# A hybrid decoder block on one Trainium2 core: later low parts, other pairs without blocks and a reordered end in the first feed-forward product

## The chip, the cores and the metric

The kernel runs on one core of a Trainium2 chip. The metric is the device time of one execution in microseconds; a run is one execution, and the time of a kernel is the median of its runs. The engines are named as the profile names them: PE is TensorE, DVE VectorE, ACT ScalarE, POOL GpSimd, and SP is SyncE, whose queue triggers most DMAs.

## What is computed

The block is a token mixer (retention and dilated attention, gated and merged) followed by a feed-forward network, each with a residual. The change lies in the feed-forward part alone, for 1024 tokens, a width of 1024 and 4096 hidden columns:

```python
def squared_relu_mlp(h, w1, w2):
    return jnp.square(jax.nn.relu(h @ w1)) @ w2

h = modulate(rms_norm(x, norm2_g[l]), sh2, sc2)
x = x + g2[:, None, :] * squared_relu_mlp(h, w_ff1[l], w_ff2[l])
return rms_norm(x, norm_f_g)
```

## The kernel before

**Split numbers.** Every operand of a matmul is split into a high part (rounded to TensorE's fast 32-bit type) and a low part (the rest). The high part is a copy on ScalarE, the low part a subtraction on VectorE, which needs the copy. One block product then takes three matmuls for each 128 rows (`mm3`, lines 219, 221 and 223): low weight by high input, high by low, high by high. Since line 219 comes first, a block product starts only when the low part of the weight is there.

**Seven products instead of eight.** `Blocks` (line 232 on) computes a 2 by 2 block product with seven block products and sums of blocks. For the first feed-forward matrix the 4096 hidden columns are worked through as 16 pairs `q` of 128 + 128 columns, and each pair needs seven products in the order 11, s1, s3, s2, 12, 22, s4 (`ORDER`). A product is 12 matmuls of 128x128 by 128x512. The names with an s use sums of weight blocks (`fs`, line 261, on VectorE).

For a product, `prep` forms the weight: the sum on VectorE if there is one, the copy of the high part on ScalarE (line 266), and the low part on VectorE (line 276), which is not issued at once but held in `self.low` until `flush`. `mm` issues the matmuls; `post` takes the result out of PSUM (line 298 a copy on ScalarE, lines 305 to 310 on VectorE, and `f_out` at lines 2218 to 2222, which adds, applies relu and squares). Product 22 adds into the PSUM bank that s3 has written and that the post of s2 must have read first (line 306 or 310).

`run` goes through `items`, the list of (pair, product): matmuls, then `prep` for as many later products as there are free tiles, then a flush, then `post`, then the callback `after`. The post of s2 is in `ahead`: it comes before the preps, and the flush is left out in the item before it. The order on each engine is the order of the code; nothing reorders it.

**ff1.** The first products of pairs 0 and 1 are woven into the normalisation of the second half of the tokens, and their inputs `t1`, `22`, `t3`, `t2`, `t4` (tiles `xt`) are formed between them. Then `run` takes the rest: (2, 11), (2, s1), then product 22 of pairs 0 and 1, whose input `t4` is the last to be formed, then (2, s3) and on to (15, s4).

**The second matrix** takes its inputs, the hidden activations `a`, from DRAM. Part of it works by blocks again: for these pairs `a_sums` (lines 2237 to 2242) forms sums of the activations on VectorE, four steps in two parts for each pair, and four pairs are one strip `c` of `xs_d`; three strips (`NS`) make 12 pairs, 0 to 11. The four other pairs, 12 to 15, are stored plainly in `a_d` and multiplied without blocks. `pack` orders the rows of the second matrix to match.

**The end of ff1.** While pair 15 runs, `second_ahead` prepares the head of the second product: `b_load(i)` triggers two loads `b{i}0`, `b{i}1` of its inputs, `b_x` splits them (line 2410 the high part on ScalarE, line 2406 the low part on VectorE), `b_raw` loads weights, `b_w` forms and splits weight sums (`w2s`, line 2448). `x1_load` (line 2104) reloads the residual into `x1r` tiles. All these loads are triggered by SP, in order; a trigger whose buffer is not free holds back those behind it. The tile tag `g0` with eight buffers serves the raw weights of ff1, its outputs `a` and the x1 tiles alike, so an x1 load can have to wait until an output is stored.

Of the kernel before, what the change touches and what calls it, by code (L numbers as in the profile page):

```python
# [133 lines left out]
def block_kernel(ctx, tc, io, stop=None, dbg=None):  # L134
# [103 lines left out]
    class Blocks:  # L238
# [79 lines left out]

        def run(self, items, sums, before=lambda q, n: None, after=lambda q, n: None, ahead=()):

            items_ahead = lambda i: i + 1 < len(items) and items[i + 1][1] in ahead
            for i, (q, n) in enumerate(items):
                before(q, n)
                self.mm(q, n)
                if n in ahead:
                    self.post(q, n)
                while sums and len(self.slots) > 1:
                    self.prep(sums.pop(0))  # L330
                if not items_ahead(i):
                    self.flush()
                if n not in ahead and n != "s1":
                    self.post(q, n)
                after(q, n)
# [1846 lines left out]

    NS = 3
    a_d = {t: dram.tile([P, S], F32, name=f"ad{t}") for t in range(8 * NS, 2 * NQ)}
# [26 lines left out]
    def f_out(q, n, x, y=None):  # L2211
# [11 lines left out]
        if n in ("12", "21"):  # L2223
            r = M["out", q][i]
            if q >= 4 * NS:
                nc.sync.dma_start(a_d[2 * q + i], r)
            elif i == 0:
                nc.sync.dma_start(xs_d[q // 4][:, 0, q % 4], r[:, :512])
            else:
                nc.sync.dma_start(xs_d[q // 4][:, 1:3, q % 4], r.rearrange("p (t x) -> p t x", t=2))  # L2230

    def a_sums(q, part):
# [11 lines left out]
        nc.sync.dma_start(xs_d[q // 4][:, 3 + 2 * part:5 + 2 * part, q % 4], r)  # L2244

# [18 lines left out]
    def ff1(ahead):  # L2264
# [71 lines left out]
        BF.post(0, "12")  # L2336
        BF.post(1, "s2")
        l()
        low = t4(3)
        BF.post(0, "s4")  # L2340
        low()
# [30 lines left out]

        BF.run(items, sums[3:], before, after, ("s2",))
        x1_load(6, x1_d)
# [97 lines left out]
    def second_ahead(n):  # L2472
# [241 lines left out]
def pack(x, c, w_ada, b_ada, norm1_g, w_in, rel_bias, ret_gn_g, ret_gn_b,  # L2714
# [51 lines left out]
```

## Time and profile before

| what | us |
|---|---|
| median of 3 runs (2180.87 to 2184.65) | 2182.93 |
| the profiled execution | 2182.82 |
| its span, from the first to the last instruction | 2181.1 |
| PE busy | 2147.4 (98%) |
| DVE busy | 1479.0 (68%) |
| ACT busy | 947.1 (43%) |
| mean granted clock of TensorE | 0.998 |

The first matmul of ff1 starts at 1534.34 us in the profiled execution, the first of the second matrix at 1848.91. A row of the timeline has the start in us, the duration, the engine, the line and operation, output and inputs by the program's names with their numbers left out, the shape, and in brackets the idle time before it and what ended it. Matmuls overlap, so the distance from start to start tells their pace, not the duration. In a row of the waits stand the total, the number of times and the longest. A row of the table of windows gives the window, its length, the busy time of PE, PEld (weight loads), DVE, ACT and POOL with the number of instructions, the granted clock of TensorE as a share of full speed, the DMA share and GB/s. SPq rows are triggers of DMAs; their second number is the time that SP spent on them, with its waits.

### The profile page before, as it was taken

Reading aid. Unit: us, or ns where it says so; the run is one execution under the profiler, and the core shown is the slowest. Engines: PE = TensorE matmul, PEld = TensorE weight load, DVE = VectorE, ACT = ScalarE, POOL = GpSimd, SP = SyncE. Lnnn points to the kernel's source line nnn. Section 1 sums busy time; section 2 is a strip of 40 time slices with the busy share of each in tenths; the row PEclk is TensorE's granted clock in tenths of the full one; section 3 lists DMA queues with packets and bytes.
Section 4 is the critical chain, followed back from the end, with each engine's and each line's share of the span. In section 5 each row is a group of like instructions: output and inputs, shape, how many; then the busy total and the mean of one; then the engine's idle time right before and its main releaser. Section 6 shows DMA issues by size and latency. Waiting matters only on the chain.

```text
span 2181.1 us, 27045 instructions
## 1 busy us (share of the span) xinstructions
PE 2147.4 (98%) x10034; PEld 1784.6 (82%) x10034; DVE 1479.0 (68%) x2281; ACT 947.1 (43%) x1715; POOL 178.4 (8%) x192
## 2 busy tenths in 40 slices
PE   7999999999999999999999999999999999999998
PEld 5888888888888888888888888888878888788887
DVE  6756777767566678854655644677876665887855
ACT  4533322333334566654644525434554455433412
POOL 0101111100000334410000000001000000000003
PEclk9999999999999999999999999999999999999999
DMA  9869998734687758977323366653054445645322
GB/s 382 231 193 297 289 328 266 217 136 155 223 297 287 257 181 242 263 222 186 105 81 108 98 250 210 224 184 130 35 202 159 154 143 188 240 138 173 109 87 78
DMA packets 161891, 422.55 MB, mean 194 GB/s; under 512 B 27734, under 2 KB 55645, under 8 KB 157662
## 3 DMA queue, kind: packets, MB, share of 16 engines
q1 hardware_dynamic: 151902, 372.57, 48.4%
q0 software_dynamic: 9856, 48.24, 10.1%
q8 instruction: 79, 1.29, 0.2%
q14 instruction: 54, 0.44, 0.1%
HBM read 325.71 MB, written 160.32 MB: 223 GB/s over the span
## 4 chain that ended last, share of the span: by engine, by line
PE 90%; DVE 4%; ACT 2%; DMA 1%; issue 1%; POOL 0%; SPq 0%; POOLq 0%; DVEq 0%; ACTq 0%
PE qap L219 6%; PE qap L223 6%; PE qap L221 6%; PE fp L219 4%; PE fp L223 4%; PE fp L221 4%; PE ak L219 2%; PE ak L221 2%; PE ak L223 2%; PE f2a L221 2%; PE f2a L223 2%; PE f2a L219 2%; PE rg L221 1%; PE rg L219 1%; PE rg L223 1%; PE va L221 1%
## 5 line engine op out<-in xcount | busy, mean ns | idle before, releaser
L219 PE MATMUL qap<-hh,qaw 128*128 128x512 f32 x264 | 102.8, 389 | 0.1
L221 PE MATMUL qap<-hl,qaw 128*128 128x512 f32 x264 | 102.7, 389 | 0.0
L223 PE MATMUL qap<-hh,qaw 128*128 128x512 f32 x264 | 102.7, 389 | 0.0
L656 POOL TENSOR_TENSOR j<-qk,j 128x512 fp32r<-128x512 f32 x32 | 48.3, 1513 | 311.7 <-ACT j L655 311.7
L2117 POOL TENSOR_TENSOR accnf<-accnf,sqnf 128x256 f32<-128x256 f32 (+1 forms) x18 | 16.6, 921 | 613.2 <-ACT sqnf L2116 613.2
L2221 ACT ACTIVATE a<-a 128x512 f32<-128x512 f32 x48 | 30.3, 632 | 78.0 <-DVE a L2220 78.0
L219 PEld LDWEIGHTS qap<-hh,qaw 128*128 128x128 f32 x264 | 49.6, 188 | 10.8 <-DVE qat L310 0.5
L221 PEld LDWEIGHTS qap<-hl,qaw 128*128 128x128 f32 x264 | 49.5, 188 | 10.3
L223 PEld LDWEIGHTS qap<-hh,qaw 128*128 128x128 f32 x264 | 49.6, 188 | 10.3
L2410 ACT CAST w2h<-w2s 128x512 fp32r<-128x512 f32 x36 | 22.4, 621 | 78.2 <-DVE w2s L2448 78.2
L2117 POOL TENSOR_TENSOR accn<-accn,sqn 128x512 f32<-128x512 f32 x12 | 15.5, 1294 | 496.0 <-ACT sqn L2116 496.0
L276 DVE TENSOR_TENSOR fw<-w1r,fw 128x512 fp32r<-128x512 f32 x48 | 32.9, 688 | 33.2 <-ACT fw L266 33.2
L1531 ACT ACTIVATE P<-P,ng 128x128 f32<-128x128 f32 (+1 forms) x96 | 41.9, 438 | 29.5 <-DVE ng L1528 29.5
L276 DVE TENSOR_TENSOR qaw<-wa,qaw 128x512 fp32r<-128x512 f32 x66 | 45.0, 686 | 11.1 <-ACT qaw L266 11.1
L1309 DVE SCALAR_TENSOR_TENSOR cossin<-cossin,cb 128x1024 f32<-128x1024 f32 x32 | 39.0, 1220 | 16.4 <-DMA cossin<-in_w_ada_dram 16.4
L219 PE MATMUL fp<-h2h,fw 128*128 128x512 f32 x128 | 50.0, 390 | 0.0
L1955 DVE TENSOR_TENSOR rwl<-rwl,rwh 128x1024 fp32r<-128x1024 f32 x25 | 30.2, 1221 | 29.0 <-ACT rwh L1985 29.0
L221 PE MATMUL fp<-h2l,fw 128*128 128x512 f32 x128 | 49.8, 389 | 0.0
L223 PE MATMUL fp<-h2h,fw 128*128 128x512 f32 x128 | 49.8, 389 | 0.0
L219 PE MATMUL roa<-rh,rwl 128*128 128x512 f32 x128 | 49.8, 389 | 0.0
L221 PE MATMUL roa<-rl,rwh 128*128 128x512 f32 x128 | 49.8, 389 | 0.0
L223 PE MATMUL roa<-rh,rwh 128*128 128x512 f32 x128 | 49.8, 389 | 0.0
(3093 smaller groups left out, 7138.1 us busy)
## 6 DMA issues: line engine op xcount, KB each, us to landing
cossin<-in_w_ada_dram SPq DMA_DIRECT2D x32, 512.0 KB, 5.3
v<-vd SPq DMA_DIRECT2D x32, 512.0 KB, 5.7
w1r<-in_w_ff_dram SPq DMA_DIRECT2D x32, 512.0 KB, 4.8
vd<-vo SPq DMA_DIRECT2D x24, 512.0 KB, 6.3
xsd<-as SPq DMA_DIRECT2D x24, 512.0 KB, 2.8
w2r<-in_w_ff2s_dram SPq DMA_DIRECT2D x24, 512.0 KB, 7.6
em<-in_w_ada_dram SPq DMA_DIRECT2D x16, 512.0 KB, 10.2
wrvs<-in_w_rv_dram POOLq DMA_DIRECT2D x16, 512.0 KB, 11.1
```

The source lines that it names most:

```text
L219: nc.tensor.matmul(o, wl, xh, start=first, stop=False, skip_group_check=skip)
L221: nc.tensor.matmul(o, wh, xl, start=False, stop=False, skip_group_check=skip)
L223: nc.tensor.matmul(o, wh, xh, start=False, stop=last, skip_group_check=skip)
L276: nc.vector.tensor_sub(t[:, 512:], src, fv(t[:, :512]))
L656: nc.gpsimd.tensor_sub(t[:, 1], src, fv(t[:, 0]))
L1309: nc.vector.scalar_tensor_tensor(t, t, 1.0, cb, op0=ALU.mult, op1=ALU.mult, accum_out=mods[:, j:j + 1])
L1531: nc.scalar.activation(v, v, AF.Exp, bias=ng[:, blk:blk + 1], accum_out=st[:, g, blk, 2 + a:3 + a])
L1955: nc.vector.tensor_sub(lo, fv(lo), fv(hi))
L2117: (nc.vector if f == 7 else nc.gpsimd).tensor_add(G["acc", key], G["acc", key], sq)
L2221: nc.scalar.activation(o, o, AF.Relu)
L2410: nc.scalar.copy(hi, src)
```

## The change

Four things, all around `ff1`. First, `run` gets a flag `lazy`: while there are sums left to prepare, the flush behind a product is left out, so that a low part is issued on VectorE behind the copy for the next weight. Second, the weight of (2, s2) is prepared before `run`, and the list of items starts with four products of pair 2 (11, s1, s3, s2) ahead of product 22 of pairs 0 and 1. Third, the pairs without blocks are 0, 1, 14 and 15, by `Q0 = 2`; pairs 2 to 13 make up the strips. Fourth, around the end the x1 loads are triggered one at a time during pairs 14 and 15, `b_load(1)` comes behind product 12 of the last pair, `b_load(2)` ahead of the last two x1 loads, and `b_x(0, .)` and half of `b_w(1, .)` later.

```diff
@@ run
-                if not items_ahead(i):
+                if not items_ahead(i) and not (lazy and sums):
                     self.flush()
@@
-    NS = 3
+    NS, Q0 = 3, 2
@@ f_out
-            if q >= 4 * NS:
-                nc.sync.dma_start(a_d[2 * q + i], r)
+            c, m = divmod(q - Q0, 4)
+            if not 0 <= c < NS:
+                nc.sync.dma_start(a_d[2 * q + i + (8 * NS if q < Q0 else 0)], r)
             elif i == 0:
-                nc.sync.dma_start(xs_d[q // 4][:, 0, q % 4], r[:, :512])
+                nc.sync.dma_start(xs_d[c][:, 0, m], r[:, :512])
...
@@ ff1
         BF.post(1, "s2")
+        BF.prep((2, "s2"))
         l()
         low = t4(3)
+        BF.flush()
         BF.post(0, "s4")
...
-        items = sums[:2] + [(0, "22"), (1, "22")] + sums[2:]
+        items = sums[:4] + [(0, "22"), (1, "22")] + sums[4:]
...
-            if q == NQ - 1 and n in ("s2", "12"):
-                for f in range(3):
-                    x1_load(f + 3 * (n == "12"), x1_d)
-
-        late = {(0, "22"): (0, 0), (1, "22"): (1, 0), (2, "s2"): (0, 1), (2, "12"): (1, 1)}
-        late.update({(q + 1, n): (q, part) for q in range(2, 4 * NS) for part, n in enumerate(("11", "s1"))})
+            f = {(2, "s2"): 0, (2, "12"): 2, (1, "s3"): 4, (1, "s2"): 1, (1, "12"): 3, (1, "22"): 5}.get((NQ - q, n))
+            if f is not None:
+                x1_load(f, x1_d)
+
+        late = {(q + 1, n): (q, part) for q in range(Q0, Q0 + 4 * NS) for part, n in enumerate(("11", "s1"))}
...
-        BF.run(items, sums[3:], before, after, ("s2",))
+        BF.run(items, sums[4:], before, after, ("s2",), True)
+        b_load(2)
         x1_load(6, x1_d)
         x1_load(7, x1_d)
         b_x(1, 0)
@@ second_ahead
         elif n == "s3":
             b_raw(0, "22", 1)
+        elif n == "s2":
             b_x(0, 0)
+        elif n == "12":
+            b_load(1)
             b_x(0, 1)
-        elif n == "12":
-            for p in range(4):
-                b_w(1, p)
+            b_w(1, 0)
+            b_w(1, 1)
         elif n == "22":
-            b_load(1)
+            b_w(1, 2)
+            b_w(1, 3)
@@ ff2_blocks
             if i == 0:
-                b_load(2)
@@ pack
-        "w_ff2": _k4(A(w_ff2)[0, 3072:]),
-        "w_ff2s": _quads(A(w_ff2)[0, :3072]),
+        "w_ff2": _k4(np.concatenate([A(w_ff2)[0, :512], A(w_ff2)[0, 3584:]])),
+        "w_ff2s": _quads(A(w_ff2)[0, 512:3584]),
```

The number of instructions on each engine stays the same. Line numbers behind the change are two to six higher. Three places show what moves.

VectorE, at the turn to pair 2, up to the post of (2, s2) at lines 309 and 310. `fw2s3` is the weight of product s3 of pair 2, `fs` a weight sum, `a0` to `a3` the outputs of pairs 0 and 1, `as` the sums of `a_sums`, `xt` the inputs, `ft2nacc` the post. Both listings follow the same row, the output step of a3 that reads `ft1h2t`; before, 24 rows lie from it to line 310, and these are the last 12 of them:

```order
L276 TENSOR_TENSOR fw311_13380<-w1r31_13320,fw311_13380 128x512
L2220 TENSOR_TENSOR a1_13284<-fp03_13211,ft0nsq_13046 128x512
L2237 TENSOR_TENSOR as00_13387<-a0_13283 128x512
L2238 SCALAR_TENSOR_TENSOR as00_13387<-as00_13387,a1_13284 128x512
L261 TENSOR_TENSOR fs3_13403<-w1r32_13322 128x512
L276 TENSOR_TENSOR fw3s1_13405<-fs3_13403,fw3s1_13405 128x512
L2220 TENSOR_TENSOR a3_13301<-fp13_13224,ft1nsq_13067 128x512
L2237 TENSOR_TENSOR as10_13412<-a2_13300 128x512
L2238 SCALAR_TENSOR_TENSOR as10_13412<-as10_13412,a3_13301 128x512
L261 TENSOR_TENSOR fs3_13403<-w1r32_13322,w1r31_13320 128x512
L309 TENSOR_TENSOR ft2nacc_13348<-ft2nacc_13348,fp22_13432 128x512
L310 TENSOR_TENSOR ft2nacc_13349<-fp23_13416,ft2nacc_13348 128x512
```

Now 14 rows, the first six and the other eight:

```order
L261 TENSOR_TENSOR fs2_13035<-fs2_13035,w1r21_12901 128x512
L276 TENSOR_TENSOR fw2s3_13071<-fs2_13035,fw2s3_13071 128x512
L2261 TENSOR_TENSOR xt42_13293<-x1_5_12199,xt42_13293 128x512
L2326 SCALAR_TENSOR_TENSOR x1_7_12201<-x1_7_12201,mods_73 128x512
L276 TENSOR_TENSOR fw2s2_13306<-fs2_13035,fw2s2_13306 128x512
L2220 TENSOR_TENSOR a0_13283<-ft0nsq_13046,fp01_13123 128x512
```

```order
L2261 TENSOR_TENSOR xt43_13311<-x1_7_12201,xt43_13311 128x512
L2220 TENSOR_TENSOR a2_13300<-ft1nsq_13067,fp11_13136 128x512
L276 TENSOR_TENSOR fw212_13342<-w1r21_12901,fw212_13342 128x512
L261 TENSOR_TENSOR fs2_13035<-fs2_13035,w1r21_12901 128x512
L276 TENSOR_TENSOR fw222_13344<-w1r22_12941,fw222_13344 128x512
L276 TENSOR_TENSOR fw2s4_13364<-fs2_13035,fw2s4_13364 128x512
L309 TENSOR_TENSOR ft2nacc_13347<-ft2nacc_13347,fp22_13383 128x512
L310 TENSOR_TENSOR ft2nacc_13348<-fp23_13367,ft2nacc_13347 128x512
```

The sums `as00` and `as10`, the second output steps of a1 and a3 and the work for pair 3's weights (`fs3`, `fw3s1`, `fw311`) are no longer ahead of line 310; the low parts of (2, s3) and (2, s2) stand near the front.

VectorE during the last pair; `w2l` is a low part of the second matrix's first weights, `b00l` and `b01l` its first inputs. Before:

```order
L2406 TENSOR_TENSOR w2l02_15309<-w2r0111_15239,w2h02_15308 128x512
L2406 TENSOR_TENSOR w2l03_15313<-w2r0111_15239,w2h03_15312 128x512
L2406 TENSOR_TENSOR b00l_15278<-b00l_15278,b00h_15331 128x1024
L309 TENSOR_TENSOR ft15nsq_15274<-ft15nsq_15274,fp152_15343 128x512
L310 TENSOR_TENSOR ft15h2t_15275<-fp153_15316,ft15nsq_15274 128x512
L2220 TENSOR_TENSOR a31_15359<-ft15h2t_15275,fp151_15284 128x512
L2448 TENSOR_TENSOR w2s00_15383<-w2r0210_15282,w2r0220_15299 128x512
L2406 TENSOR_TENSOR b01l_15280<-b01l_15280,b01h_15334 128x1024
```

Now:

```order
L2410 TENSOR_TENSOR w2l02_15313<-w2r0111_15242,w2h02_15312 128x512
L309 TENSOR_TENSOR ft15nsq_15278<-ft15nsq_15278,fp152_15339 128x512
L310 TENSOR_TENSOR ft15h2t_15279<-fp153_15322,ft15nsq_15278 128x512
L2220 TENSOR_TENSOR a31_15355<-ft15h2t_15279,fp151_15288 128x512
L2410 TENSOR_TENSOR w2l03_15317<-w2r0111_15242,w2h03_15316 128x512
L2410 TENSOR_TENSOR b00l_15282<-b00l_15282,b00h_15359 128x1024
L2452 TENSOR_TENSOR w2s00_15385<-w2r0210_15286,w2r0220_15303 128x512
L2410 TENSOR_TENSOR b01l_15284<-b01l_15284,b01h_15382 128x1024
```

The post of (15, s2), the rows of `ft15nsq` and `ft15h2t`, has moved ahead of the low part of `b00l`.

SP's queue at the end of ff1; `x1r_6` is an x1 load, `b10l` a load of an input of the second matrix, `ad31` a store of an output of pair 15. Before:

```order
L2104 DMA x1r_4_15365<-x1d4_254 128x1024
L2104 DMA x1r_5_15367<-x1d5_255 128x1024
L2226 DMA ad31_265<-a31_15359 128x1024
L2424 DMA b10l_15423<-xsd0_266 128x1024
L2424 DMA b11l_15425<-xsd0_266 128x1024
L2226 DMA ad30_264<-a30_15358 128x1024
L2104 DMA x1r_6_15443<-x1d6_256 128x1024
L2104 DMA x1r_7_15445<-x1d7_257 128x1024
L2424 DMA b20l_15453<-xsd0_266 128x1024
L2424 DMA b21l_15455<-xsd0_266 128x1024
```

Now:

```order
L2104 DMA x1r_1_15337<-x1d1_251 128x1024
L2104 DMA x1r_3_15362<-x1d3_253 128x1024
L2428 DMA b10l_15378<-xsd0_266 128x1024
L2428 DMA b11l_15380<-xsd0_266 128x1024
L2104 DMA x1r_5_15397<-x1d5_255 128x1024
L2227 DMA ad31_265<-a31_15355 128x1024
L2227 DMA ad30_264<-a30_15354 128x1024
L2428 DMA b20l_15443<-xsd0_266 128x1024
L2428 DMA b21l_15445<-xsd0_266 128x1024
L2104 DMA x1r_6_15447<-x1d6_256 128x1024
L2104 DMA x1r_7_15449<-x1d7_257 128x1024
L2404 DMA w2r0120_15457<-in_w_ff2s_dram 128x1024
```

`b10l` and `b11l` stand ahead of both stores, `b20l` and `b21l` behind the stores and ahead of `x1r_6` and `x1r_7`.

More of the change, by code (lines that the diff above doesn't have):

```diff
@@ L317, in post, with run @@
                 self.out(q, "12", u, d)
-        def run(self, items, sums, before=lambda q, n: None, after=lambda q, n: None, ahead=()):
+        def run(self, items, sums, before=lambda q, n: None, after=lambda q, n: None, ahead=(), lazy=False):
             items_ahead = lambda i: i + 1 < len(items) and items[i + 1][1] in ahead
@@ L2224, in f_out @@
             r = M["out", q][i]
-            if q >= 4 * NS:
-                nc.sync.dma_start(a_d[2 * q + i], r)
+            c, m = divmod(q - Q0, 4)
+            if not 0 <= c < NS:
+                nc.sync.dma_start(a_d[2 * q + i + (8 * NS if q < Q0 else 0)], r)
             elif i == 0:
-                nc.sync.dma_start(xs_d[q // 4][:, 0, q % 4], r[:, :512])
+                nc.sync.dma_start(xs_d[c][:, 0, m], r[:, :512])
             else:
-                nc.sync.dma_start(xs_d[q // 4][:, 1:3, q % 4], r.rearrange("p (t x) -> p t x", t=2))
+                nc.sync.dma_start(xs_d[c][:, 1:3, m], r.rearrange("p (t x) -> p t x", t=2))
     def a_sums(q, part):
@@ L2243, in a_sums @@
                                            op1=ALU.subtract)
-        nc.sync.dma_start(xs_d[q // 4][:, 3 + 2 * part:5 + 2 * part, q % 4], r)
+        c, m = divmod(q - Q0, 4)
+        nc.sync.dma_start(xs_d[c][:, 3 + 2 * part:5 + 2 * part, m], r)
     BF = Blocks("f", X, ["g1"] * 4 + ["att*"] * 4 + ["att"] * 2 + ["att*"] * 2 + ["wh", "wl"] * 3,
```

## The prediction

> **What bounds the kernel now.** I read the page first: its busy table and its chain that ended last.
>
> ```profile
> span 2181.1 us, 27045 instructions
> PE 2147.4 (98%) x10034; PEld 1784.6 (82%) x10034; DVE 1479.0 (68%) x2281; ACT 947.1 (43%) x1715; POOL 178.4 (8%) x192
> PE 90%; DVE 4%; ACT 2%; DMA 1%; issue 1%; POOL 0%; SPq 0%; POOLq 0%; DVEq 0%; ACTq 0%
> ```
>
> TensorE carries 98% of the span and the chain runs through it for 90%. The diff changes no matmul, so it can only give back time in which TensorE stood still or ran slowly. Next I asked who TensorE waited for in the stretch that the diff touches, from the first feed-forward matmul (1534 us) to the third product of the second (1881 us):
>
> ```profile
> PE fp L219 <- DVE ft2nacc L310: 3.3, 1, 3.3
> PE f2a L221 <- DVE b21l L2406: 1.1, 1, 1.1
> PE fp L219 <- DVE ft15h2t L310: 0.8, 1, 0.8
> PE n21ss L381 <- DVE accn L2117: 0.3, 1, 0.3
> ```
>
> No other row stands there, and the last one, of the norm, is untouched. So a handful of microseconds is all that can be won. What a stall costs is read from start to start, because matmuls overlap. The clean pace: pair 9's product s1 starts at 1717.21 and its s2, two products or 24 matmuls later, at 1722.65, so 0.227 us for a matmul and 2.72 us for a product of 12.
>
> ```profile
> 1710.53 0.69 DVE L276 TENSOR_TENSOR fw9s<-fs,fw9s 128x512 fp32r<-128x512 f32 x1 [0.67 <-ACT fw9s L266]
> 1717.21 0.39 PE L219 MATMUL fp<-xt10h,fw9s 128*128 128x512 f32 x1
> 1722.65 0.39 PE L219 MATMUL fp<-xt,fw9s 128*128 128x512 f32 x1
> ```
>
> The large stall, in the timeline of TensorE, and the granted clock behind it, in the table of windows:
>
> ```profile
> 1589.34 0.39 PE L223 MATMUL fp<-h2h,fw 128*128 128x512 f32 x1
> 1593.02 0.50 PE L219 MATMUL fp<-xt,fw 128*128 128x512 f32 x1 [3.29 <-DVE ft2nacc L310]
> ...
> 1594.40 0.63 PE L223 MATMUL fp<-xt,fw 128*128 128x512 f32 x1
> ...
> 1597.39 0.48 PE L219 MATMUL fp<-x220h,fw2s 128*128 128x512 f32 x1
> 1597.71 0.39 PE L221 MATMUL fp<-x220l,fw2s 128*128 128x512 f32 x1
> 1575.00:1589.00 14.00, 14.00 (x63) 11.58 (x63) 10.82 (x18) 10.05 (x18) 0.00 (x0) 1.00 0.34 128
> 1594.40:1597.00 2.60, 2.60 (x8) 2.01 (x7) 1.94 (x4) 2.57 (x5) 0.00 (x0) 0.50 0.13 46
> ```
>
> From 1589.34 to 1597.71 are 14 matmul starts, 8.37 us where 14 x 0.227 = 3.18 would do: **5.19 us lost**. 3.45 of it is the wait itself (3.68 less one pace); the other 1.74 is the clock, granted at 0.50 for 2.6 us after it, when the starts come 0.43 apart.
>
> The Trainium skill has a rule for this ("TensorE: Matmul & The Clock Gate", Part 1: The HAM clock gate): after about one idle window of some 3.4 us the array falls to half clock, and a like time of activity brings it back. The 0.50 row behind the 3.68 us gap agrees; the return 4.4 us after the restart does too.
>
> **The change, part by part.**
>
> *(a) The stall at pair 2.* TensorE waited at product (2, 22) for L310, the step of VectorE that reads that PSUM bank. VectorE was simply late:
>
> ```profile
> 1573.91 0.69 DVE L2220 TENSOR_TENSOR a<-fp,ft1h2t 128x512 f32<-128x512 f32 x1
> ...
> 1577.82 0.68 DVE L261 TENSOR_TENSOR fs<-fs,w1r 128x512 f32<-128x512 f32 x1
> 1578.42 0.69 DVE L276 TENSOR_TENSOR fw2s<-fs,fw2s 128x512 fp32r<-128x512 f32 x1
> 1580.67 0.69 DVE L276 TENSOR_TENSOR fw2s<-fs,fw2s 128x512 fp32r<-128x512 f32 x1 [1.57 <-ACT fw2s L266]
> ...
> 1592.27 0.69 DVE L310 TENSOR_TENSOR ft2nacc<-fp,ft2nacc 128x512 f32<-128x512 f32 x1
> 1575.97 0.39 PE L219 MATMUL fp<-xt,fw 128*128 128x512 f32 x1
> ```
>
> Between a3's step (1573.91) and L310 VectorE has 24 rows before and 14 now: ten move behind L310 (the four first steps of pair 0's and 1's block sums, two output steps, two weight sums and two low parts of pair 3). Rows follow each other at 0.60 us (1577.82 to 1578.42), so L310 moves up by 10 x 0.60 = 6.0 us even if every wait for ScalarE stays, such as the 1.57 in the row of 1580.67. It then ends at 1592.96 - 6.0 = 1587.0 or sooner; TensorE arrives at 1589.34 + 0.23 = 1589.57. Margin at least 2.6 us: the wait goes, and with it the slow clock. Its own input is no hindrance: (2, s2) is now the fourth product and ends two products after 1575.97, at 1581.4. Term: **-5.19**. If the cover failed by 1 us, 1 us would come back.
>
> What is late next is the third product. Products (0, 22) and (1, 22) now follow (2, s2), so at 1575.97 TensorE needs the low part of (2, s3) instead. In the row order it stands second behind a3's step: 1573.91 + 2 x 0.60 + 0.69 = 1575.80. Margin 0.17 us, the tightest place of the change. (2, s2), due at 1578.69, has its low part three rows later; 1.0 us of margin if ScalarE's copy comes in time, and 0.4 us for the bank that the output step behind it frees. No row of before shows this order, so bounds: from 0 to the wait if the low part stayed at its place of before, 1578.42 + 0.69 - 1575.97 = 3.14 us. I take 0.1, because the rows ahead of it are all short steps whose inputs are there. Term: **+0.1** (0 to 3.1).
>
> *(b) Low parts one product later, everywhere.* With `lazy`, a low part is no longer flushed in the product that copied its high part but behind the next copy, about one product (2.72 us) later, so that VectorE no longer stands waiting for ScalarE. The rows above give the cover: pair 9's s2 has its low part at 1710.53 + 0.69 = 1711.22 and TensorE reads it at 1722.65, 11.4 us later. 8.7 us remain. Term: **0**; if the cover were gone, each of 13 pairs would wait.
>
> *(c) Which pairs go without blocks.* Pairs 0, 1, 14, 15 now, 12 to 15 before: the eight sum steps of VectorE leave pairs 0 and 1, whose VectorE is late, and come back in pairs 12 and 13. Pairs 2 to 11 carried the same steps before, and the waits above show no wait of TensorE there. The stores stay as many bytes. Term: **0** besides what (a) counts.
>
> *(d) The end of the stage.* Two places, both on VectorE's row order and on SP's queue:
>
> ```profile
> 1840.71 1.23 DVE L2406 TENSOR_TENSOR b00l<-b00l,b00h 128x1024 fp32r<-128x1024 f32 x1 [4.44 <-ACT b00h L2410]
> 1842.57 0.69 DVE L310 TENSOR_TENSOR ft15h2t<-fp,ft15nsq 128x512 f32<-128x512 f32 x1
> 1842.10 0.39 PE L223 MATMUL fp<-h2h,fw 128*128 128x512 f32 x1
> 1843.32 0.50 PE L219 MATMUL fp<-xt,fw 128*128 128x512 f32 x1 [0.83 <-DVE ft15h2t L310]
> 1843.65 0.40 PE L221 MATMUL fp<-xt,fw 128*128 128x512 f32 x1
> ...
> 1859.79 0.39 PE L219 MATMUL f2c<-b10h,w2l 128*128 128x512 f32 x1
> 1860.58 0.40 PE L223 MATMUL f2c<-b10h,w2h 128*128 128x512 f32 x1
> 1861.51 0.39 PE L219 MATMUL f2c<-b11h,w2l 128*128 128x512 f32 x1
> 1862.32 0.40 PE L223 MATMUL f2c<-b11h,w2h 128*128 128x512 f32 x1
> 1872.77 0.39 PE L219 MATMUL f2a<-b21h,w2l 128*128 128x512 f32 x1
> 1874.57 0.40 PE L223 MATMUL f2a<-b21h,w2h 128*128 128x512 f32 x1
> ```
>
> At (15, 22) TensorE loses 1843.65 - 1842.10 - 2 x 0.227 = 1.10 us, because L310 stood behind b00l's low part, and that behind a load. Now L309 and L310 stand ahead of b00l; they can start when (15, s2) ends, one product (2.72 us) before (15, 22), and need 1.4: margin 1.3. Term: **-1.10**. At b10l, b11l and b21l the same sum gives 0.34, 0.36 and 1.35 us. Their loads in SP's queue:
>
> ```profile
> 1837.43 6.33 SPq L2104 DMA_DIRECT2D x1r<-x1d  x6
> ...
> 1852.61 0.38 SPq L2424 DMA_DIRECT2D b10l<-xsd  x1
> ...
> 1853.94 0.38 SPq L2226 DMA_DIRECT2D ad<-a  x1
> 1855.29 6.45 SPq L2104 DMA_DIRECT2D x1r<-x1d  x2
> 1861.84 0.38 SPq L2424 DMA_DIRECT2D b20l<-xsd  x1
> ```
>
> b20l was issued at 1861.84 because SP had stood 6.45 us at x1r_6 and x1r_7, whose buffers are free only when pair 15's output is stored. It now goes ahead of them, directly behind that store: about 1854.4, 7.4 us earlier, for 1.35 us of lateness. b10l and b11l move ahead of both stores of pair 15 and are asked for one product sooner; only 0.34 and 0.36 are wanted. Term: **-2.05**. Late next would be x1r_6 and x1r_7, issued 0.9 us later behind the two b loads; the step that first reads them stands behind b21l's low part on VectorE, so they cannot bring that stall back. The six other x1 loads took 6.33 us of SP in one row and now go one by one. Two of them stand ahead of b00l: 2.1 us at that rate, 6.5 at that of x1r_6 and x1r_7. b00l's low part ended at 1841.94, and the second matrix starts two products after 1843.32, at 1848.8, so 6.9 us cover both ends: 0. The weight sums of the second product, which trade places with output steps, are due a whole product (10.9 us, four blocks) after that: 0.
>
> Sum: -5.19 + 0.1 - 1.10 - 2.05 = **-8.24**. The profiled execution took 2182.82 us (span 2181.1 and 1.7 around it), 0.11 below the median of the three runs; against that median the forecast is 2182.93 - 8.2 = **2174.7 us**.
>
> **The rivals.**
>
> *A new wait at (2, s3).* For it: a margin of 0.17 us, and a copy on ScalarE ahead of the next low part. Against it: only two short steps stand ahead. Full price 3.1 us, 2177.8; if a wait of that length brought the slow clock in the row's proportion (5.19 to 3.45), 4.7 us, 2179.4.
> By the clock rule named above a wait under 3.4 us costs only itself, which would give the first of the two figures.
>
> *The end of the stage keeps its stalls.* For it: the same bytes go through the same queue in the same 30 us, and b00l, b10l wait for a landing and not only for their issue. Then only (a) counts: 2182.9 - 5.1 = 2177.8.
>
> *The change does not do what it says at pair 2:* if VectorE is held by the waits for ScalarE or for pair 3's weights and not by its count of rows, L310 stays late. Then only (d) counts: 2182.9 - 3.15 = 2179.8. Against it: the ten rows are behind L310 in the program itself.
>
> *Slower.* The low parts come so late that TensorE waits for one in each of the 13 pairs from 3 on, at s2, whose low part now follows the copy of 12. One step of VectorE late (0.69 us) costs 13 x 0.69 = 9.0 us and gives 2183.7; two steps, 17.9 us and 2192.6. It decides from 8.2 / 13 = 0.63 us a pair. Against it stand 8.7 us of margin in each.
>
> **How the numbers follow.** Forecast 0.73; a new wait of over 1 us 0.08; the end kept 0.09; pair 2 kept 0.05; slower 0.03; others 0.02. A measurement of this kernel tells 0.2%, 4.4 us, from no change. Faster by more than that are the forecast, the end kept, and most of the new waits: 0.87. Within it: pair 2 kept and the rest of the waits, 0.09. Slower 0.04. Low end: all 8.3 us and the lowest run's 2.1 below the median, 2172.5. High end: 2178.5, above the two rivals at 2177.8 and short of the one at 2179.8.
>
> **What would show it.** Right: no row for ft2nacc, ft15h2t or b21l among TensorE's waits from 1534 to 1875, no window at 0.50 in the stage, L310 of pair 2 done before 1587, starts at 0.227 through (2, s3); b20l issued right behind pair 15's stores. Wrong: a wait of fp at L219 for fw2s3 or fw2s2 near 1576 to 1579; a wait of f2a for b00l or b01l; a regular wait of some tenths once in 19 us, which would be the low parts.

## The result, and the profile after

| | before | after |
|---|---|---|
| median of the runs, us | 2182.93 (7 runs, 2180.87 to 2184.88) | 2175.77 (7 runs, 2174.99 to 2178.76) |
| profiled execution: span, us | 2181.1 | 2174.0 |
| first matmul of ff1 | 1534.34 | 1535.71 |
| first matmul of the second matrix | 1848.91 | 1843.94 |
| ff1 (between the two) | 314.57 | 308.23 |
| second matrix to the span's end | 332.19 | 330.06 |

The ratio is 0.9968, with a 95% interval from 0.9959 to 0.9977: 7.2 us, or 0.3%, faster. The prediction said 2174.7 (2172.5 to 2178.5).

In the two profiled executions ff1 has become 6.34 us shorter and what follows it 2.13, together 8.47. The span shows 7.1 of it, because ff1 started 1.37 us later in that execution, in a stretch where the programs are the same (in the fourteen profiles of this study it starts between 1534.34 and 1536.02). So the kernels below are compared by two numbers: the median over the runs, and the time from ff1's first matmul to the span's end in the profiled execution, which is 646.76 before and 638.29 after.

The page of the changed kernel, its busy table and its chain:

```profile
span 2174.0 us, 27035 instructions
PE 2144.1 (99%) x10034; PEld 1782.9 (82%) x10034; DVE 1478.5 (68%) x2281; ACT 948.3 (44%) x1715; POOL 176.8 (8%) x192
PE 94%; DVE 3%; ACT 1%; issue 0%; DMA 0%; POOL 0%; POOLq 0%; DVEq 0%; ACTq 0%
```

TensorE's busy time has fallen by 3.3 us with the same 10034 matmuls: those are the slow ones that are gone, and its share of the chain has risen from 90% to 94%. Who TensorE waits for in the stretch in which four rows stood before (1530 to 1880 us):

```profile
PE n21ss L381 <- DVE accn L2117: 0.3, 1, 0.3
```

Only the untouched row of the norm is left. The windows over the place where the clock had been at 0.50 (columns as before):

```profile
1586.00:1600.00 14.00, 14.00 (x63) 11.62 (x62) 11.18 (x18) 9.76 (x17) 0.00 (x0) 1.00 0.52 180
1600.00:1625.00 25.00, 25.00 (x112) 20.67 (x112) 18.43 (x29) 12.84 (x23) 0.00 (x0) 1.00 0.70 256
```

TensorE is busy throughout, at full clock. VectorE's rows, from a3's step to the step that pair 2's product 22 had waited for, in the timeline:

```profile
1575.28 0.69 DVE L2220 TENSOR_TENSOR a<-fp,ft1h2t 128x512 f32<-128x512 f32 x1
1575.89 0.68 DVE L261 TENSOR_TENSOR fs<-fs,w1r 128x512 f32<-128x512 f32 x1
1576.49 0.68 DVE L276 TENSOR_TENSOR fw2s<-fs,fw2s 128x512 fp32r<-128x512 f32 x1
...
1578.36 0.68 DVE L276 TENSOR_TENSOR fw2s<-fs,fw2s 128x512 fp32r<-128x512 f32 x1
...
1583.85 0.69 DVE L276 TENSOR_TENSOR fw<-w1r,fw 128x512 fp32r<-128x512 f32 x1 [3.01 <-ACT fw L266]
...
1586.44 0.68 DVE L309 TENSOR_TENSOR ft2nacc<-ft2nacc,fp 128x512 f32<-128x512 f32 x1
1587.15 0.69 DVE L310 TENSOR_TENSOR ft2nacc<-fp,ft2nacc 128x512 f32<-128x512 f32 x1
...
1607.50 0.69 DVE L309 TENSOR_TENSOR ft3nsq<-ft3nsq,fp 128x512 f32<-128x512 f32 x1 [1.12 <-PE fp L223]
1608.23 0.69 DVE L310 TENSOR_TENSOR ft3h2t<-fp,ft3nsq 128x512 f32<-128x512 f32 x1
```

And TensorE's where these are read, at (2, s3), at (2, 22) and at (3, 22):

```profile
1577.34 0.40 PE L219 MATMUL fp<-xt,fw2s 128*128 128x512 f32 x1
...
1590.98 0.39 PE L219 MATMUL fp<-xt,fw 128*128 128x512 f32 x1
...
1610.02 0.39 PE L219 MATMUL fp<-xt,fw 128*128 128x512 f32 x1
```

The low part of (2, s3) ends at 1576.49 + 0.68 = 1577.17 and is read at 1577.34: the margin of 0.17 us that was forecast, to the hundredth. L310 of pair 2 ends at 1587.84, 3.1 us ahead of its reader, though VectorE stood 3.01 us for a copy of ScalarE on the way, a wait that the prediction did not have. In pair 3 L309 already waits for TensorE and not the other way round (1.12 us in its bracket): VectorE has caught up, with 1.1 us from the end of L310 (1608.92) to the start of (3, 22).

SP's queue at the end of ff1:

```profile
1846.91 3.48 SPq L2227 DMA_DIRECT2D ad<-a  x2
1850.50 0.37 SPq L2428 DMA_DIRECT2D b20l<-xsd  x1
1851.27 0.43 SPq L2428 DMA_DIRECT2D b21l<-xsd  x1
1851.80 1.76 SPq L2104 DMA_DIRECT2D x1r<-x1d  x2
```

b20l is triggered right behind pair 15's two stores, 6.6 us after the second matrix has begun, where it had been 12.9 us (1861.84 less 1848.91). The two x1 loads behind it take SP 1.76 us instead of 6.45.

### The profile page after: what moved, and what is told of

Same layout as the page of the kernel before. It is cut to its first block, busy times and chain, and to the rows that moved or that the text cites. A ratio compares the mean times of both kernels' runs of the same rounds, so it can differ in the third digit from the quotient of the medians.

```text
span 2174.0 us, 27035 instructions
## 1 busy us (share of the span) xinstructions
PE 2144.1 (99%) x10034; PEld 1782.9 (82%) x10034; DVE 1478.5 (68%) x2281; ACT 948.3 (44%) x1715; POOL 176.8 (8%) x192
## 4 chain that ended last, share of the span: by engine, by line
PE 94%; DVE 3%; ACT 1%; issue 0%; DMA 0%; POOL 0%; POOLq 0%; DVEq 0%; ACTq 0%
PE qap L219 6%; PE qap L223 6%; PE qap L221 6%; PE fp L219 5%; PE fp L221 5%; PE fp L223 5%; PE f2a L221 2%; PE f2a L223 2%; PE f2a L219 2%; PE ak L219 2%; PE ak L221 2%; PE ak L223 2%; PE rg L221 1%; PE rg L219 1%; PE rg L223 1%; PE va L223 1%
## 5 line engine op out<-in xcount | busy, mean ns | idle before, releaser
L266 ACT CAST qaw<-wa 128x512 fp32r<-128x512 f32 x66 | 39.6, 616 | 23.7 <-PE qap L223 15.3
```

The source lines that it names most:

```text
L266: nc.scalar.copy(t[:, :512], src)
```

## The experiments

The question was not whether TensorE's waits are gone, which the profile shows, but which of the four parts removed which wait, and whether the prices that the prediction gave them hold: item order with VectorE's lighter row order -5.19, low parts later 0, other pairs without blocks 0, the end -3.15. So each part was made alone, each was left out alone, and the place with the tightest margin was loaded. "ff1 to end" is the time from ff1's first matmul to the span's end, in the one execution that was traced. Each ratio is to runs of the kernel before that were made beside it (their medians lie between 2182.87 and 2183.42).

| kernel | median (range), us | ratio to before (95%) | ff1 to end | waits of TensorE over 1 us: product, us |
|---|---|---|---|---|
| before | 2182.93 | 1 | 646.76 | (2, 22) 3.3; b21l 1.1 |
| the change | 2175.77 (2174.99 to 2178.76) | 0.9968 (0.9959 to 0.9977) | 638.29 | none |
| order alone | 2187.31 (2184.41 to 2188.45) | 1.0016 (1.0007 to 1.0026) | 650.76 | (3, 12) 2.4; (3, 22) 3.7 |
| low parts alone | 2179.18 (2178.01 to 2183.28) | 0.9982 (0.9973 to 0.9992) | 642.68 | (2, 22) 1.9 |
| pairs alone | 2182.83 (2181.29 to 2184.8) | 0.9998 (0.9988 to 1.0008) | 646.80 | (2, 22) 2.9 |
| pairs alone, loads earlier | 2180.49 (2178.93 to 2184.49) | 0.9991 (0.9981 to 1.0) | 643.86 | (2, 22) 1.2; b21l 1.7 |
| end alone | 2181.21 (2180.41 to 2183.3) | 0.9991 (0.9981 to 1.0) | 644.35 | (2, 22) 3.3 |
| without low parts | 2181.96 (2180.39 to 2184.19) | 0.9995 (0.9986 to 1.0005) | 645.99 | (3, 22) 3.7 |
| without pairs | 2181.26 (2178.4 to 2182.68) | 0.9993 (0.9983 to 1.0002) | 645.41 | (3, 22) 3.7 |
| without order | 2176.49 (2175.82 to 2177.2) | 0.9973 (0.9962 to 0.9984) | 640.07 | (2, 22) 1.6 |
| without end | 2176.82 (2175.86 to 2178.1) | 0.9972 (0.9961 to 0.9983) | 639.82 | none (b21l 0.6) |

**Order alone.** The kernel before with the fourth product ahead of product 22 of pairs 0 and 1, and its weight prepared early; the sums of pairs 0 and 1 are two products later for that.

```diff
+        BF.prep((2, "s2"))
...
-        items = sums[:2] + [(0, "22"), (1, "22")] + sums[2:]
+        items = sums[:4] + [(0, "22"), (1, "22")] + sums[4:]
-        late = {(0, "22"): (0, 0), (1, "22"): (1, 0), (2, "s2"): (0, 1), (2, "12"): (1, 1)}
+        late = {(0, "22"): (0, 0), (1, "22"): (1, 0), (2, "12"): (0, 1), (2, "22"): (1, 1)}
```

> The kernel before with one part of the change: the weight of (2, s2) is prepared ahead of the loop and products (2, s3) and (2, s2) go ahead of product 22 of pairs 0 and 1; the sums of pairs 0 and 1 stay, two products later. Theory V (VectorE's queue is late by a fixed number of rows, and each of the three parts takes rows or waits out of it): the wait at (2, 22) goes, but the sums and the weights of pair 3 that stood ahead of line 310 are still to be done, so the lateness comes back within one pair, as waits of 2 to 4 us at pair 3; total from 2180 to 2188 us. Theory O (the order alone removes the stall, since it gives line 310 two more products of time): no wait above 0.3 us in pairs 2 and 3, total 2182.9 - 5.2 = 2177.7 us.

The timelines of ScalarE and TensorE at pair 3:

```profile
1607.23 0.63 ACT L2221 ACTIVATE a<-a 128x512 f32<-128x512 f32 x1 [1.35 <-DVE a L2220]
1609.57 0.50 PE L219 MATMUL fp<-h2h,fw 128*128 128x512 f32 x1 [2.44 <-ACT ft3nsq L298]
...
1612.19 0.39 PE L223 MATMUL fp<-h2h,fw 128*128 128x512 f32 x1
1616.24 0.79 PE L219 MATMUL fp<-xt,fw 128*128 128x512 f32 x1 [3.66 <-DVE ft3h2t L310]
1616.83 0.63 PE L221 MATMUL fp<-xt,fw 128*128 128x512 f32 x1
1617.26 0.63 PE L223 MATMUL fp<-xt,fw 128*128 128x512 f32 x1
...
1621.10 0.61 PE L223 MATMUL fp<-xt,fw 128*128 128x512 f32 x1
```

Slower than before. The wait at pair 2 is gone, and VectorE's lateness comes due one pair later, twice: 2.44 us at (3, 12), by way of a copy of ScalarE (L298) that stood behind steps waiting for VectorE, such as the row of 1607.23, and 3.66 at (3, 22), followed by starts 0.43 us apart for 5 us. The item order gives VectorE no time; it puts L310 of pair 2 ahead of ten rows, and these rows now stand ahead of pair 3's.

**Low parts alone, pairs alone, end alone.** The kernel before with the flag `lazy` set; with the pairs 0, 1, 14 and 15 plain; with the new triggers at the end.

```diff
-        BF.run(items, sums[3:], before, after, ("s2",))
+        BF.run(items, sums[3:], before, after, ("s2",), True)
```

> The kernel before with the lazy flush alone. V: the waits of VectorE for ScalarE ahead of line 310 (1.57 + 0.69 + 0.74 = 3.0 us) shrink, the rows stay; the wait at (2, 22) falls from 3.45 to between 0.4 and 1.9 us and the slow clock behind it goes; total 2178 to 2180 us. O: nothing changes at pair 2, 2182.9 us.

The waits of TensorE with the low parts later and nothing else:

```profile
PE fp L219 <- DVE ft2nacc L310: 1.9, 1, 1.9
PE f2a L221 <- DVE b21l L2406: 0.8, 1, 0.8
PE f2c L221 <- DVE b10l L2406: 0.6, 1, 0.6
```

This one edit takes 1.4 us off the wait at (2, 22), behind which no slow clock follows now, and removes the wait for ft15h2t at (15, 22), where the prediction gave the whole 1.10 us to the reordered end.

```diff
-    NS = 3
+    NS, Q0 = 3, 2
...
-        late = {(0, "22"): (0, 0), (1, "22"): (1, 0), (2, "s2"): (0, 1), (2, "12"): (1, 1)}
-        late.update({(q + 1, n): (q, part) for q in range(2, 4 * NS) for part, n in enumerate(("11", "s1"))})
+        late = {(q + 1, n): (q, part) for q in range(Q0, Q0 + 4 * NS) for part, n in enumerate(("11", "s1"))}
```

> The kernel before with the other choice of pairs without blocks alone (0, 1, 14, 15). V: four sum rows of 0.6 us leave the queue ahead of line 310; the wait at (2, 22) falls from 3.45 to between 0.8 and 2.0 us, the slow clock goes; total 2178.5 to 2180 us. O: nothing changes at pair 2, 2182.9 us.

A miss: 2.86 us of wait where 0.8 to 2.0 were expected, and no gain. Three engines in the timelines of this kernel, SP's queue, ScalarE and VectorE:

```profile
1578.56 2.65 SPq L2227 DMA_DIRECT2D ad<-a  x2
1581.31 1.20 SPq L2194 DMA_DIRECT2D w1r<-in_w_ff_dram  x2
1586.24 0.62 ACT L266 CAST fw<-w1r 128x512 fp32r<-128x512 f32 x1 [1.68 <-DMA w1r<-in_w_ff_dram]
1586.89 0.69 DVE L276 TENSOR_TENSOR fw<-w1r,fw 128x512 fp32r<-128x512 f32 x1 [1.60 <-ACT fw L266]
```

VectorE has four steps fewer ahead of L310, but the time goes into waits. SP stood at two stores of pair 0 and 1 (2.65 us), the loads of pair 3's weights behind them were triggered at 1581.31 (1579.38 before; 0.76 of the 1.93 us between is ff1's later start in this execution), ScalarE waited 1.68 us for the weight, and VectorE 1.60 for ScalarE's copy. Whether the stores did it was tried next: the same kernel with the two loads of pair 3 triggered ahead of them.

```diff
+        for part in (1, 2):
+            w1_load(3, part)
         low()
         BF.post(0, "12")
...
-        for part in (1, 2):
-            w1_load(3, part)
```

> q0_only with the two loads of pair 3's weights triggered ahead of the stores of a0 and a2 on SP. W: VectorE's wait of 1.60 us for the copy of fw311 goes, the wait at (2, 22) falls from 2.86 to about 1.3 us (0.8 to 1.7), and the slow clock goes with it (2.9 us in q0_only); 2182.8 - 1.6 - 2.9 = 2178.3 us. Rival (the ten rows' worth of work decides, not the load): 2182.8 us, the wait stays at 2.9.

The waits of TensorE in it:

```profile
PE fp L219 <- DVE ft2nacc L310: 1.2, 1, 1.2
PE f2a L221 <- DVE b21l L2407: 1.7, 1, 1.7
```

The wait is 1.19 us without a slow clock behind it, as expected, so it was SP's queue that had eaten the freed steps: from ff1's first matmul L310 ends after 58.6 us in the kernel before, 58.2 with the pairs alone and 56.5 here. The time is a miss, 2180.49 where 2178.3 was expected: at the end b21l cost 1.7 us in this profile, 1.3 more than where the loads stood behind the stores. Why it grew is not settled.

```diff
-            if q == NQ - 1 and n in ("s2", "12"):
-                for f in range(3):
-                    x1_load(f + 3 * (n == "12"), x1_d)
+            f = {(2, "s2"): 0, (2, "12"): 2, (1, "s3"): 4, (1, "s2"): 1, (1, "12"): 3, (1, "22"): 5}.get((NQ - q, n))
+            if f is not None:
+                x1_load(f, x1_d)
...
+        b_load(2)
         x1_load(6, x1_d)
```

> The kernel before with the reordered end alone (x1 loads one by one, b loads earlier, b00 and b01 split later). If the stalls there come from the order of the queues: no wait at (15, 22), b10l, b11l, b21l, so 3.15 us less, 2179.8 us, with pair 2 unchanged. If they come from the bandwidth that the loads share: the waits stay, 2182.9 us.

All the waits of the end vanish and (2, 22) keeps its 3.3, as expected. From the second matrix to the span's end it takes 330.01 us instead of 332.19, the 2.1 us of the prediction. The median gained 1.7 where 3.15 were expected. In the traced execution the clock is at 0.50 for 6.8 us at the wait at (2, 22) and not for 3.4 (the windows are in the last section), which gives 1.1 us back there; whether the other executions are the same in this is not on record.

**All but one part.** The changed kernel with the flag off; with the pairs 12 to 15 plain again (the sums of pairs 0 and 1 as in order alone); with product 22 of pairs 0 and 1 ahead of (2, s3) again and the weight of (2, s2) no longer prepared ahead of the loop; with the end as before.

```diff
-        BF.run(items, sums[4:], before, after, ("s2",), True)
+        BF.run(items, sums[4:], before, after, ("s2",))
```

> The changed kernel with the lazy flush taken out again. Theory W (VectorE's queue at pair 2 is late by its rows and by its in-order waits for copies on ScalarE, which themselves wait for pair 3's weights; no part alone clears both, and what is not cleared falls due at pair 3): a wait of 2 to 4 us at (3, 22), with the slow clock behind it if it is as long as the 2.86 us of q0_only; 2.3 to 7 us over the changed kernel's 2175.8, so 2178 to 2183 us. Rival (order and choice of pairs are enough, lazy is only a reserve): 2175.8 us, no wait.

> The changed kernel with pairs 12 to 15 without blocks as before, so that the eight sum rows of pairs 0 and 1 (8 x 0.61 = 4.9 us of VectorE) stand at the start of pair 3. W: a wait of 1 to 3 us at (3, 22), 2177 to 2181 us. Rival (order and lazy are enough): 2175.8 us, no wait.

> The changed kernel with product 22 of pairs 0 and 1 ahead of (2, s3) as before. W: with the sums and most of the ScalarE waits gone line 310 is late by 0.3 to 1.5 us, without slow clock; 2176 to 2177.5 us. Rival (the order is what clears pair 2): the wait of before, 2.9 us or more with the slow clock, 2180 us or more.

Both kernels that lack one of the two parts priced at 0 lose most of the gain, at pair 3. Without the other pairs the wait is longer than the 1 to 3 us that were expected, and the time just above the range. Why is seen in VectorE's groups between 1575 and 1612 us (number, busy time and mean, then the idle time ahead of them and what ended it). In the changed kernel:

```profile
L276 DVE TENSOR_TENSOR fw<-w1r,fw 128x512 fp32r<-128x512 f32 x6 | 4.1, 687 | 4.1 <-ACT fw L266 4.1
L276 DVE TENSOR_TENSOR fw3s<-fs,fw3s 128x512 fp32r<-128x512 f32 x4 | 2.7, 686 | 0.4 <-ACT fw3s L266 0.3
```

Without the later low parts:

```profile
L276 DVE TENSOR_TENSOR fw<-w1r,fw 128x512 fp32r<-128x512 f32 x6 | 4.1, 690 | 7.7 <-ACT fw L266 7.7
L276 DVE TENSOR_TENSOR fw3s<-fs,fw3s 128x512 fp32r<-128x512 f32 x4 | 2.8, 692 | 3.5 <-ACT fw3s L266 3.5
```

Without the other pairs:

```profile
L276 DVE TENSOR_TENSOR fw<-w1r,fw 128x512 fp32r<-128x512 f32 x6 | 4.1, 685 | 3.0 <-ACT fw L266 3.0
L276 DVE TENSOR_TENSOR fw3s<-fs,fw3s 128x512 fp32r<-128x512 f32 x4 | 2.7, 686 | 0.1
L2237 DVE TENSOR_TENSOR as<-a 128x512 f32<-128x512 f32 x3 | 2.1, 685 | 0.8 <-ACT a L2222 0.8
L2241 DVE TENSOR_TENSOR as<-a,a 128x512 f32<-128x512 f32 x3 | 2.1, 685 | 1.6 <-DMA xsd<-as 1.6
```

In the one VectorE stands 7.7 + 3.5 us ahead of low parts, waiting for copies, where it stands 4.1 + 0.4 in the changed kernel; in the other it stands 3.0 + 0.1, but has the sums of pairs 0 to 2 to do (three of the first of four steps, in the row of L2237) and not those of pair 2 alone, and stands 1.6 us more ahead of the third of these steps until earlier sums are stored (L2241). Either way L310 of pair 3 is 3.7 us late, and the slow clock follows. VectorE needs both relief measures to be in time at (3, 22), and then it has the 1.1 us of margin shown above. Without the order L310 of pair 2 stands behind the steps of product 22 of pairs 0 and 1 again, and the other parts make up for all but 1.62 us of it; no slow clock follows, and 1.78 us are lost from ff1 to the end. That wait is a little longer than the 0.3 to 1.5 us that were expected; the median is in its range, and 0.7 above the changed kernel's, which is within the noise of the runs.

```diff
-            f = {(2, "s2"): 0, (2, "12"): 2, (1, "s3"): 4, (1, "s2"): 1, (1, "12"): 3, (1, "22"): 5}.get((NQ - q, n))
-            if f is not None:
-                x1_load(f, x1_d)
+            if q == NQ - 1 and n in ("s2", "12"):
+                for f in range(3):
+                    x1_load(f + 3 * (n == "12"), x1_d)
...
-        b_load(2)
         x1_load(6, x1_d)
```

> The changed kernel without its reordered end: the x1 loads again three at a time, b_load(1) and b_load(2), b_x(0, .) and b_w(1, .) where they were before; low parts, item order and pairs without blocks as in the changed kernel. Theory D (the end is worth its own term): waits of TensorE for b21l (0.6 to 1.7 us) and b10l (0.3 to 0.6) come back, from the start of the second matrix to the span's end it is 331.5 to 332.5 us where the changed kernel has 330.1, no window at half clock, time 2177.8 (2177.2 to 2178.7). The wait for ft15h2t stays away, since it was away where the low parts alone came later. Rival (the end gains only beside a late pair 2, with later low parts VectorE has room and nothing comes back): 2175.8, 330.1 us.

The waits of TensorE without the reordered end:

```profile
PE f2a L221 <- DVE b21l L2409: 0.6, 1, 0.6
```

The second matrix to the span's end takes 331.68 us, 1.6 more than in the changed kernel, and the median is 1.05 higher (2176.82, 0.4 below the range expected), with intervals that overlap. Only b21l comes back, with a wait of 0.6 us; b10l and ft15h2t do not. Of the 1.6 us, 1.1 are lost in the first 46 us of the second matrix, where b10l, b11l and b21l are read. The other 0.5 comes only in or behind the last 220 of its 1520 matmuls, and is not the end of ff1: kernels that have the reordered end show it too (330.55 us without the later low parts, 330.54 without the other pairs, where the changed kernel has 330.06). So beside later low parts the reordered end is worth about 1.1 us in the profiles, and not 3.15.

**The tightest place, loaded.** The low part of (2, s3) is subtracted one, four or six times more, with the same result, so that VectorE is late by a chosen amount at the place with 0.17 us of margin.

```diff
-                nc.vector.tensor_sub(t[:, 512:], src, fv(t[:, :512]))
+                for _ in range(5 if (self.name, q, n) == ("f", 2, "s3") else 1):
+                    nc.vector.tensor_sub(t[:, 512:], src, fv(t[:, :512]))
```

> The changed kernel with the low part of the third matrix's first block (2,s3) subtracted one extra time (the same values, 0.60 us more on VectorE; the output does not change). In the changed kernel this low part ends 0.17 us ahead of the matmul that reads it. Theory M (that margin is what the profile says): a wait of 0.60 - 0.17 = 0.4 us at the first product with s3 of pair 2, no slow clock, time 2176.2 (2175.5-2177). Rival R (the margin is not real, the matmul's order gives more room): no wait there, 2175.8.

> As the run with one extra subtraction, with four: 2.4 us more on VectorE ahead of the same matmul. Theory M: a wait of 4 x 0.60 - 0.17 = 2.2 us. Theory G (a wait of up to 2.44 us was followed by no slow clock in the runs so far, one of 2.86 us by 5 us at half clock): no slow clock after it, time 2178.1 (2177.3-2179.3). Rival P (each us waited costs 1.5 us, as the 3.45 us at pair 2 of the kernel before cost 5.19): 2179.2 and starts 0.43 us apart after the wait.

> With six extra subtractions: 3.6 us more on VectorE. Theory M: a wait of 6 x 0.60 - 0.17 = 3.4 us. Theory G: it is past the point, so 2.6 to 6 us of starts 0.43 us apart follow and cost 1.2 to 2.9 us more: 2180.5-2182.2, a step of 2.4 to 4.1 us over the run with four extra subtractions where VectorE's own addition is 1.2. Rival P: 2181.0, a step of 1.8. Rival Q (the wait alone costs, and the clock's fall belongs to the place and not to the wait's length): 2179.3, a step of 1.2, no starts 0.43 apart.

| extra subtractions | median (range), us | ratio to before (95%) | wait at (2, s3) | ff1 to end |
|---|---|---|---|---|
| 0 | 2175.77 (2174.99 to 2178.76) | 0.9968 (0.9959 to 0.9977) | none | 638.29 |
| 1 | 2175.8 (2175.07 to 2176.6) | 0.9968 (0.9955 to 0.9981) | 0.48 | 638.94 |
| 4 | 2178.24 (2177.81 to 2179.45) | 0.9976 (0.9967 to 0.9986) | 2.64 | 641.66 |
| 6 | 2181.36 (2180.54 to 2182.26) | 0.9994 (0.9985 to 1.0003) | 4.10 | 644.48 |

VectorE and TensorE with four extra subtractions:

```profile
1575.43 3.59 DVE L277 TENSOR_TENSOR fw2s<-fs,fw2s 128x512 fp32r<-128x512 f32 x5
1579.08 0.50 PE L219 MATMUL fp<-xt,fw2s 128*128 128x512 f32 x1 [2.64 <-DVE fw2s L277]
1579.42 0.40 PE L221 MATMUL fp<-xt,fw2s 128*128 128x512 f32 x1
1579.66 0.40 PE L223 MATMUL fp<-xt,fw2s 128*128 128x512 f32 x1
```

And TensorE with six:

```profile
1581.88 0.80 PE L219 MATMUL fp<-xt,fw2s 128*128 128x512 f32 x1 [4.10 <-DVE fw2s L277]
1582.48 0.63 PE L221 MATMUL fp<-xt,fw2s 128*128 128x512 f32 x1
1582.90 0.63 PE L223 MATMUL fp<-xt,fw2s 128*128 128x512 f32 x1
```

The margin is what the profile said. The repeats follow each other at 0.725 us (3.59 us for five, the last of 0.69) and not at 0.60, and with that the waits should be 0.55, 2.7 and 4.2 us; they are 0.48, 2.64 and 4.10. Price: four cost 2.5 us in the median for 2.6 of wait, with starts back at 0.24 directly behind it; six cost 5.6 us, of which 4.26 are the gap beyond one pace (1577.39 to 1581.88, less 0.23) and the rest starts 0.43 apart. The step from four to six is 3.1 us where VectorE's addition is 1.45. That is as theory G had it; a price in proportion to the wait fails at four, and a wait that costs only itself fails at six. Theory G's reason, a limit on the length of the wait, is a different matter (last section). With one extra the profile shows the 0.6 us more from ff1 to the end, and the medians do not tell it.

## Why the prediction was right, and where its working was not

*(a) The stall at pair 2, -5.19 and +0.1.* Right in mechanism, and in size for the execution that it was read from. L310 was to end at 1587.0 or sooner; it ended at 1587.84, which is 1586.47 in the time of the execution before, since ff1 began 1.37 us later. The wait and the slow clock are gone. The +0.1 for the new third product was 0: the margin of 0.17 was real, and held. ff1 became 6.34 us shorter; -5.19 + 0.1 - 1.10 = -6.19 was forecast. The slow clock was read as 2.6 us, the length of the window that was asked for; the trace has it at 0.50 for 3.4 us. And the term is not the same in every execution: with the end alone the same wait of 3.30 us had 6.8 us of slow clock at it.

The rival that was named there, a new wait at (2, s3), did not come. Brought about by four extra subtractions, a wait of 2.64 us at that place cost about its own length (2178.24), as the first of its two figures had it; one of 4.10 us, by six, cost more (2181.36). The rule beside those figures, by which a wait under 3.4 us costs only itself, failed elsewhere: 2.86 us in the kernel with the pairs alone and 3.29 in the kernel before were followed by the half clock. The prediction had seen the rule agree because it held 3.68 us against it, the distance from start to start, and not the 3.29 in which TensorE was idle.

*(b), (c) Later low parts and other pairs, 0 each.* They cost nothing, as the terms said, but that they bring nothing was wrong, and here the working stopped short. The step counted ten rows that move behind L310 of pair 2 and asked what is late next only at the third product, not where those ten rows are done: ahead of L310 of pair 3. In the kernel with the order alone they are late there, by 3.7 us. The parts priced at 0 are what VectorE pays this debt with, and each is needed: leaving one out loses 7.7 or 7.1 us from ff1 to the end (0.5 of it, in both, at the end of the span, as in the kernel without the reordered end), and 6.2 or 5.5 us in the median. By the prediction's terms a kernel without the later low parts would have taken the same 2174.7 us; it took 2181.96. That the sum came out in spite of this was luck: the change happened to contain both parts, and they cover pair 3 with 1.1 us to spare. A sum of the four parts made alone gives, from ff1 to end, 4.00 - 4.08 + 0.04 - 2.41 = -2.45 us; together they give -8.47. The sentence that pairs 2 to 11 carried the same sums without waits was right for the sums' new place, pairs 12 and 13, where no wait came.

*(d) The end, -3.15.* The waits went as forecast, b20l was triggered 6.4 us earlier after the second matrix's start (7.4 written), and the second matrix shrank by 2.13 (2.05 written). The 1.10 at (15, 22) is not the end's alone: later low parts remove it by themselves, and beside them the reordered end is worth about 1.1 us.

*The sum.* -8.24 against -8.47 in the two profiles, and 7.2 in the medians; 2174.7 was written and 2175.77 measured. The 1 us between is within the range of the runs and of ff1's start; what it comes from stays open.

*The slower rival,* low parts late in every pair, did not come: with the low parts alone later, TensorE waits for none of ff1's weights.

## What to carry to other kernels

When an engine is late at one reader, moving its work behind that reader moves the lateness to the next one: count the rows and waits up to the second reader too, and ask what makes the engine itself faster. Parts of a change that each seem to cost and bring nothing can be the ones that carry it, so leave each out alone as well as trying it alone. A wait of TensorE can cost more than its length: here those that left it idle for less than about 1.6 us of any one 3.41 us window of the clock cost only themselves, and those that left it idle for more than about 1.8 cost 1.5 to 2.9 us more.

## What the runs showed of the hardware

**The half clock.** Eleven profiles have twelve waits of TensorE over 1 us in ff1. Behind those of 1.19, 1.62, 1.87, 2.44 and 2.64 us the matmuls went on at full pace. At those of 2.86, 3.29, 3.30, 3.66, 3.67, 3.74 and 4.10 us the granted clock fell to 0.50, with starts 0.43 us apart, and that cost 1.5 to 2.9 us on top of the wait.

This looks like a limit on the wait's length, between 2.64 and 2.86 us. But the granted clock of the traces has a grid beneath it. It was at 0.50 for 3.41 us in two profiles (the kernel before, and six extra subtractions) and for 6.83 in the five others, and in these seven traces the time from its end to the next fall, near the end of the span, is a whole multiple of 3.413 us (576.85 us, or 169 times, in the kernel before: from 1597.59 to 2174.44). Where the clock stayed in ff1, the grid can be counted back from that last fall. Four windows: the two windows of the grid in which the order alone has most of its waits of 2.44 and 3.66 us, then the half clock of the kernel before and of the end alone:

```profile
1607.90:1611.31 3.41, 1.75 (x8) 1.45 (x9) 2.21 (x4) 1.61 (x3) 0.00 (x0) 1.00 1.02 394
1611.32:1614.73 3.41, 1.26 (x6) 0.72 (x4) 2.72 (x5) 0.62 (x1) 0.00 (x0) 1.00 1.04 398
1594.18:1597.58 3.40, 3.40 (x10) 2.61 (x9) 2.74 (x6) 3.05 (x7) 0.00 (x0) 0.50 0.16 60
1592.47:1599.27 6.80, 5.74 (x14) 4.50 (x15) 5.57 (x10) 4.42 (x8) 0.00 (x0) 0.50 0.47 175
```

TensorE was idle for 3.41 - 1.75 = 1.66 us of the first window, and the clock stayed; it was idle for 3.41 - 1.26 = 2.15 us of the second, and the clock fell at its end, 1.5 us before TensorE started again. The same working for all twelve waits: the clock fell behind the windows with 1.98, 2.15, 2.23, 2.26, 2.27, 2.70 and 3.41 us of idle time, and stayed where no window had more than 1.19, 1.40, 1.62, 1.62 and 1.66. At the end of the span two windows with 1.61 and 1.62 us were followed by a fall as well, so the limit lies near half a window, and none with 1.79 us or more passed in any trace. The half clock lasted one window where its first window held no more than 0.47 us of idle time, and two where that held 0.88 to 1.51.

So, as far as these traces go, the price of a wait hangs on where it lies on the grid: the 2.64 us lay across a boundary, 1.01 us in one window and 1.62 in the next. No run moved a wait of one length along the grid. The grid lies differently in each execution (a boundary at 1594.17 us in the kernel before, at 1592.46 with the end alone), and only one execution of each kernel was traced: with four extra subtractions six executions took 2177.81 to 2178.31 us, the traced one among them, and four took 2179.11 to 2179.45. Whether the clock fell in those four is not known.

The Trainium skill ("TensorE: Matmul & The Clock Gate", Part 1: The HAM clock gate) speaks of windows of about 3.4 us that run freely, so that the point of change depends on where in a window the work falls; the grid of 3.413 us agrees with it. A whole idle window of 3.4 us was not needed: 1.98 us of idle time in one window were enough. The same page, under "Why this matters for your kernels", warns of idle gaps over about 3 us; the gap of 2.86 us shows that a shorter one can be enough.

**Steps of VectorE that follow closely.** Repeating a subtraction into the same tile, VectorE took 0.725 us from one to the next, where unlike steps of the same shape follow each other at 0.60. About the same distance stands between L309 and L310 in the rows of the changed kernel (0.71 at 1586.44, 0.73 at 1607.50), where the second reads what the first has just written. No run varied this, so the cause is not shown.
